# Second block of a two-block network: the context's first norm moved into the sums over V, and attention handled by head pairs

## The chip, the core and the metric

The kernel runs on one core of a Trainium2 chip, in one launch. The metric is the time of that launch on the device in microseconds, as the median of several runs; lower is better. TensorE (PE) multiplies matrices into PSUM, VectorE (DVE) and ScalarE (ACT) work element by element, GpSimd (POOL) issues the gathers and SyncE (SP) issues all other DMAs.

## The reference, cut to what matters

The network is one block (delta rule, dilated attention, and a feed-forward of 16384 experts) on 512 tokens of width 1024, followed by a second block of two layers, on the same tokens and on a context of 256 tokens. In float32 throughout. The change touches the hand-over between the blocks and the attention of the second one:

```python
# first block, its end: 128 chosen experts per token, kept as one dense sum over all experts
h = h + peer_ffn(rmsnorm(h, norm_ffn[layer]), ...)      # gelu(x U) * gates, then times V
# second block, layer i
h  = rms_norm(x,  norm_mix[i]) * (1.0 + sc1)  + sh1
hc = rms_norm(xc, norm_mix[i]) * (1.0 + sc1c) + sh1c    # xc: the context, 256 tokens
y, yc = token_mixers(h, hc, ...)
# token_mixers: gated linear attention (4 heads), and for each of 6 + 6 heads of width 64
s_loc = einsum(q, k of the window) * scale + bias       # neighbourhood (na) or sliding window (swa)
s_ctx = einsum(q, k of the context) * scale
p = softmax(concatenate([s_loc, s_ctx]))                # swa: with a sink
o = p_loc @ v of the window + p_ctx @ v of the context
```

## The kernel before, in words

Activations lie with features on the 128 partitions and tokens along the row. A projection is 8 chunks of 128 features times three matmuls (`mm3`, L204 to L206): operands are split into a high and a low part, and the three large products are summed in a PSUM bank `ac`. A weight tile of 512 KB is loaded (`wr`), its high part made on ACT (`wh`, L142) and its low part on DVE (`wl`, L199).

The stages around the change, in order: the sums over V (`peer_v`, 128 steps of 18 matmuls, with `sparse_v` on gathered rows beside them); a tail that turns the sums (`py`) round and adds them to `x`; then `ctx0`, the context's mixers in layer 0; `wo0c`, their output projection; `mix0`, the mixers of the 512 tokens; output projection and feed-forward; and `ctx1`, `mix1` and the rest for layer 1. In `ctx1` no attention output is needed.

In `block2`, `ctx0` begins with `s.norm`: for each of 8 chunks a scale on DVE (`nt`), a shift on ACT (`xh`) and the remainder on DVE (`xl`), on 256 columns. Its inputs, the context `cx`, its reciprocal norm `early_r` and the modulation `mod[0, 1]`, have been ready since the first block. `mixers` then runs generators side by side with `interleave`: each yields an estimate of TensorE's time and a gap before it is to go on, and the generator that is due next is asked next. A scheduler in the tile framework orders the instructions of each engine from that. The generators of `mixers` are one for the gated linear attention, three that take attention units from a queue, one for the projections (a next pair of heads waits until `aq.done` says that all but two pairs are through), and, in `ctx0`, `x_entry` (two norms of `x`, the first begins with the matmul at L267) and `mods`: 48 loads `mw` of 512 KB, each used by 8 matmuls of 32 weight columns (L1165).

One attention unit is one head and one block of 128 queries (`attn_unit`): scores (L1321 to L1325), `softmax` on DVE, ACT, DVE into `pr`, then `probs_times_v`: transposes (L236), a copy on ACT into `pt`, and one product per 128 keys (L410), 64 weight columns wide, into one half of the partitions of the bank `po`:

```python
        for j in range(nb):
            s.nc.tensor.matmul(po, vs[j], pt[:, j, :], start=j == 0, stop=j == nb - 1, skip_group_check=True)
```

A unit has nb = 2 blocks of keys in `ctx0`, 4 in neighbourhood attention, and 4 (first and last query block) or 5 in sliding-window attention. There are 24 units in `ctx0` and 48 each in `mix0` and `mix1`. After all mixers the outputs are split, and the output projection follows; TensorE's order takes its first products in between the last units.

Of the kernel before, what the change touches and what calls it, by code (L numbers as in the profile page):

```python
# [23 lines left out]
CTX = 256  # L24
# [18 lines left out]
def flat(t):  # L43
    return t.rearrange("p a b -> p (a b)")
# [61 lines left out]
class Net:  # L106
# [984 lines left out]
    def peer_v(s, p0, p1, x, Hd, Gd, S, sv, keep):  # L1091
# [38 lines left out]
        interleave([sv, reload(), dense()])  # L1130
# [57 lines left out]
    def gla(s, p, T, L, pair, s0, sout, y):  # L1188
# [9 lines left out]
        for d in range(2):  # L1198
# [113 lines left out]
    def attn_unit(s, p, q, loc, ctx, sink, vs, po, after=None):  # L1312


        mm = s.nc.tensor.matmul
        lw = loc[2] if loc else 0
        b0 = s.bank()
        cps = b0[:, lw:lw + CTX] if lw + CTX <= 512 else s.bank()[:, :CTX]
        segs = [(cps, s.zero[:, 0:1].to_broadcast([128, CTX]), lw)]
        if loc:  # L1320
            mm(b0[:, :lw], q, loc[0], start=True, stop=False)  # L1321
            mm(b0[:, :lw], q, loc[1], start=False, stop=True)
            segs.append((b0[:, :lw], loc[3](), 0))
        mm(cps, q, ctx[0], start=True, stop=False)
        mm(cps, q, ctx[1], start=False, stop=True)  # L1325
# [4 lines left out]
        if after:  # L1330
            after()
# [38 lines left out]
    def mixers(s, st, i, T, xp, xh, xl, y, is_ctx, lanes=()):  # L1370
# [9 lines left out]
        def units(kind, n, make):  # L1380

            box = {"left": n}

            def po():
                if "b" not in box:
                    box["b"] = s.pob()
                return box["b"]

            def after():
                box["left"] -= 1  # L1390
                if box["left"] == 0:
                    make["out"](box["b"])
            for g in make["units"](po, after):
                aq.put(g)
# [22 lines left out]
        def na_units(pair, ks, vw, qs, ck):  # L1417
            def mk(po, after):
                for n in range(nt):
                    nb = None  # L1420
                    if not is_ctx:
                        nb = {}
                    for h in range(2):
                        hh = slice(64 * h, 64 * h + 64)
                        cv = [KV["nv"][:, j, pair * 128 + 64 * h:pair * 128 + 64 * h + 64] for j in range(2)]
                        o = lambda n=n, hh=hh: po()[hh, n * 128:(n + 1) * 128]
                        q = qs[h][:, n * 128:(n + 1) * 128]
                        if is_ctx:
                            yield s.attn_unit(p, q, None, ks[h], None, cv, o, after)
                            continue  # L1430
                        w0 = (0, 64, 192, 256)[n]

                        def bias(n=n, h=h, nb=nb):
                            if "t" not in nb:
                                nb["t"] = s.t(p, "nbias", [128, 2, 256], 2)
                                nc.sync.dma_start(nb["t"], s.I["nabias"][i, n, :, 2 * pair:2 * pair + 2, :])
                            return nb["t"][:, h]
                        vs = [vw[:, n, j, hh] for j in range(2)] + cv
                        yield s.attn_unit(p, q, (ks[h][0][:, w0:w0 + 256], ks[h][1][:, w0:w0 + 256], 256, bias),
                                          ck[h], None, vs, o, after)  # L1440
            return mk

        def swa_units(pair, ks, vt, qs, ck):
            def mk(po, after):
                for n in range(nt):
                    for h in range(2):
                        head = 2 * pair + h
                        kv = head // 3
                        hh, vh = slice(64 * h, 64 * h + 64), slice(64 * kv, 64 * kv + 64)
                        cv = [KV["sv"][:, j, vh] for j in range(2)]  # L1450
                        q = qs[h][:, n * 128:(n + 1) * 128]
                        o = lambda n=n, hh=hh: po()[hh, n * 128:(n + 1) * 128]
                        sk = s.sink[:, head:head + 1]
                        if is_ctx:
                            yield s.attn_unit(p, q, None, ks[kv], sk, cv, o, after)
# [3 lines left out]
                        yield s.attn_unit(p, q, (ks[kv][0][:, lo * 128:hi * 128], ks[kv][1][:, lo * 128:hi * 128], w,  # L1459
                                                 lambda c0=c0, w=w: s.c2["swam"][:, c0:c0 + w]), ck[kv], sk,  # L1460
                                          [vt[:, j, vh] for j in range(lo, hi)] + cv, o, after)
# [4 lines left out]
        def proj_lane():  # L1466
            for kind, m in seq:
# [3 lines left out]
                if kind in ("nk", "sq") and y is not None:  # L1471
                    left = aq.put_pairs - 2
                    yield lambda left=left: aq.done >= left * 2 * nt
# [48 lines left out]
                elif kind == "nq":  # L1522
                    pair = m - 9
                    qs = s.q_parts(p, s.evac(p, ps, "ra", T, bufs=2, scale=0.125, grid=not is_ctx), T, "qp")
                    units(kind, 2 * nt, dict(units=na_units(pair, A["k"], A["v"], qs, A.get("ck")),
# [18 lines left out]
                elif kind == "sq":  # L1544
# [3 lines left out]
                    units(kind, 2 * nt, dict(units=swa_units(pair, A["sk"], A["sv"], qs, A.get("sck")),  # L1548
# [13 lines left out]
        interleave([gq.lane(), aq.lane(), aq.lane(), aq.lane(), *lanes, proj_lane()])  # L1562
# [133 lines left out]
    def block2(s, x):  # L1696
# [3 lines left out]
        with ExitStack() as st:  # L1700
# [11 lines left out]
            with ExitStack() as t:  # L1712
                s.mark("ctx0")
                xc, np_ = s.pool(t, "xc"), s.pool(t, "np")
# [3 lines left out]
                ch = s.norm(np_, xc, cx, mc[0][:, 8:16], CTX, mc[0][:, 0:8], s.early_r)  # L1718
                with ExitStack() as t2:
                    s.mixers(t2, 0, CTX, xc, *ch, cx, True, [s.x_entry(np_, x, gain, xp, mx[0], xs),  # L1720
# [7 lines left out]
                s.early_r = s.rstd(s.early, CTX)  # L1728
            for i in range(2):
# [194 lines left out]
def network(st, tc, I):  # L1924
# [5 lines left out]
    s.early = s.pool(st, "early")  # L1930
# [20 lines left out]
```

## Time and profile before

| | |
|---|---|
| median of 3 runs | 4083.6 us (4079.09 to 4084.34) |
| the profiled execution | 4080.38 us, its span 4078.6 us |
| TensorE busy | 3921.0 us, 96% of the span |
| VectorE busy | 2324.0 us, 57% |
| ScalarE busy | 1573.6 us, 39% |
| mean granted TensorE clock | 0.988 of full speed |

Busy is the time in which an engine had at least one instruction under way. Matmuls overlap, so the distance from one start to the next is what a matmul costs in a stream, not its own duration. A product of two float32 operands that were not split stands in the trace as two records (two passes). In the second block the stages lie at about 2228 to 2400 us (`ctx0`), 2400 to 2424 (`wo0c`), 2424 to 2713 (`mix0`), 3305 to 3385 (`ctx1`) and 3385 to 3656 (`mix1`).

### The profile page before, as it was taken

To read this page: it belongs to the slowest core of one execution; us is meant where nothing else is said; L and a number is where in the kernel's file an instruction comes from. 1 tells how busy PE (TensorE), PEld (TensorE's weight loads), DVE (VectorE), ACT (ScalarE), POOL (GpSimd) and SP (SyncE) were. 2 spreads that over 40 slices of the span, in tenths; PEclk is the share of its full clock that TensorE was granted. 3 is DMA by queue.
4 is the path that set the end of the run, shared out by engine and by line. 5 is a ranking of instruction groups with operands and counts; after the bars stand their busy time and mean duration, and the time that the engine had idled before them with its cause. 6 is when DMAs were issued, how large, how long until landed. Compare 5 with 4: busy or idle time off the path is not lost.

```text
span 4078.6 us, 57929 instructions
## 1 busy us (share of the span) xinstructions
PE 3921.0 (96%) x22491; PEld 3316.5 (81%) x22491; DVE 2324.0 (57%) x5133; ACT 1573.6 (39%) x2776; POOL 325.7 (8%) x287
## 2 busy tenths in 40 slices
PE   8999999999878999989998999999999999999998
PEld 5878988789877899766887778888888888887887
DVE  7526544569998776434556757663222266664334
ACT  5335454433223333323333645553121245553222
POOL 0000000004445310222000000000000000000000
PEclk9999999999998999999999999999999999999999
DMA  5342132338889876988764651121212141122332
GB/s 196 106 150 74 37 99 98 113 115 321 316 293 326 319 266 236 339 287 308 257 217 163 241 198 43 58 83 63 67 63 62 60 127 58 55 86 78 95 96 83
DMA packets 218594, 637.62 MB, mean 156 GB/s; under 512 B 25552, under 2 KB 65360, under 8 KB 214736
## 3 DMA queue, kind: packets, MB, share of 16 engines
q1 hardware_dynamic: 181456, 499.69, 36.3%
q0 software_dynamic: 36864, 134.23, 9.1%
q8 instruction: 177, 2.90, 0.3%
q14 instruction: 97, 0.79, 0.1%
HBM read 575.12 MB, written 58.72 MB: 155 GB/s over the span
## 4 chain that ended last, share of the span: by engine, by line
PE 54%; DMA 8%; DVE 6%; issue 1%; ACT 1%; POOL 0%; DVEq 0%; SPq 0%; ACTq 0%; POOLq 0%
PE ac L205 13%; PE ac L206 13%; PE ac L204 13%; DMA pa<-Hd 6%; PE po L410 3%; PE bk L995 2%; DVE wl L199 2%; PE bk L236 2%; PE bk L205 1%; PE bk L204 1%; PE bk L206 1%; DVE pl L145 1%; DMA wr<-V 1%; PE bk L1321 1%; PE bk L1165 1%
## 5 line engine op out<-in xcount | busy, mean ns | idle before, releaser
L204 PE MATMUL ac<-xh,wh 128*128 128x512 f32 (+2 forms) x3608 | 1301.6, 362 | 54.2 <-ACT h L136 41.2
L206 PE MATMUL ac<-xh,wl 128*128 128x512 f32 (+2 forms) x3608 | 1280.8, 356 | 14.1 <-DVE wl L199 13.8
L205 PE MATMUL ac<-xl,wh 128*128 128x512 f32 (+2 forms) x3608 | 1282.0, 356 | 1.0 <-DVE xl L148 0.7
L142 ACT ACTIVATE wh<-wr 128x1024 fp32r<-128x1024 f32 (+1 forms) x599 | 630.4, 1054 | 1618.9 <-PE ac L205 1173.4
L199 DVE TENSOR_TENSOR wl<-wr,wh 128x1024 fp32r<-128x1024 f32 (+1 forms) x599 | 726.9, 1214 | 557.4 <-ACT wh L142 529.8
L204 PEld LDWEIGHTS ac<-xh,wh 128*128 128x128 f32 x3608 | 683.8, 190 | 160.5 <-ACT h L136 51.7
L206 PEld LDWEIGHTS ac<-xh,wl 128*128 128x128 f32 x3608 | 683.8, 190 | 96.4 <-DVE wl L199 20.7
L205 PEld LDWEIGHTS ac<-xl,wh 128*128 128x128 f32 x3608 | 684.7, 190 | 79.8 <-issue 7.8
L145 DVE TENSOR_TENSOR pa<-pa,pg 128x384 f32<-128x384 f32 x128 | 66.1, 555 | 298.1 <-DMA pa<-Hd 292.0
L205 PE MATMUL bk<-wl,ph 128*128 128x512 f32 x512 | 201.2, 393 | 0.0
L204 PE MATMUL bk<-wh,ph 128*128 128x512 f32 x512 | 201.1, 393 | 0.0
L206 PE MATMUL bk<-wh,pl 128*128 128x512 f32 x512 | 200.6, 392 | 0.0
L205 PE MATMUL ac<-al,wh 128*128 128x512 f32 (+1 forms) x528 | 186.0, 352 | 0.0
L206 PE MATMUL ac<-ah,wl 128*128 128x512 f32 (+1 forms) x528 | 185.5, 351 | 0.0
L204 PE MATMUL ac<-ah,wh 128*128 128x512 f32 (+1 forms) x528 | 185.0, 350 | 0.0
L148 DVE SCALAR_TENSOR_TENSOR x<-ac,mod,x 128x512 f32<-128x512 f32 (+1 forms) x64 | 46.4, 726 | 186.1 <-PE ac L206 185.8
L993 DVE TENSOR_SCALAR ob<-iota,pi,pi 128x128 f32<-128x128 f32 x384 | 110.2, 350 | 72.7 <-PE bk L995 70.0
L915 POOL DMA_INDIRECT x<-Ur,rows x86 | 121.5, 1413 | 329.1 <-DVE sc L825 213.1
L145 DVE TENSOR_TENSOR nt<-ac,nt 128x512 f32<-128x512 f32 (+1 forms) x44 | 29.9, 680 | 160.2 <-PE ac L206 159.9
L142 ACT ACTIVATE ph<-pa 128x384 fp32r<-128x384 f32 x128 | 66.7, 523 | 138.8 <-DVE pa L145 61.9
L205 PE MATMUL ac<-wl,ph 128*128 128x512 f32 x256 | 101.9, 398 | 18.7 <-DVE wl L199 18.7
L915 POOL DMA_INDIRECT x<-V,rowsT x86 | 97.0, 1128 | 236.1 <-PE bk L956 212.4
(450 smaller groups left out, 5820.9 us busy)
## 6 DMA issues: line engine op xcount, KB each, us to landing
wr<-win SPq DMA_DIRECT2D x151, 512.0 KB, 3.5
wr<-U SPq DMA_DIRECT2D x128, 512.0 KB, 5.4
wr<-V SPq DMA_DIRECT2D x128, 512.0 KB, 5.8
mw<-wmod SPq DMA_DIRECT2D x96, 512.0 KB, 4.2
Hd<-h SPq DMA_DIRECT2D x64, 384.0 KB, 4.9
pa<-Hd SPq DMA_DIRECT2D x64, 384.0 KB, 5.9
Gd<-gs SPq DMA_DIRECT2D x24, 1024.0 KB, 7.5
pg<-Gd SPq DMA_DIRECT2D x21, 1152.0 KB, 7.2
```

Of the source, the lines that this page charges most:

```text
L142: s.nc.scalar.activation(out, in_, AF.Copy, **kw)
L145: s.nc.vector.tensor_tensor(out, a, b, op=op)
L148: s.nc.vector.scalar_tensor_tensor(out, a, sc, b, op0=op0, op1=op1)
L199: (eng or nc.vector).tensor_tensor(lo[:, :nk, :], raw[:, :nk, :], r32(hi[:, :nk, :]), op=ALU.subtract)
L204: mm(out, ah, bh, start=start, stop=False)
L205: mm(out, ah, bl, start=False, stop=False)
L206: mm(out, al, bh, start=False, stop=stop)
L236: s.nc.tensor.transpose(out, in_, s.ident)
L410: s.nc.tensor.matmul(po, vs[j], pt[:, j, :], start=j == 0, stop=j == nb - 1, skip_group_check=True)
L915: s.nc.gpsimd.indirect_dma_start(out=g, out_offset=None, in_=table, in_offset=bass.IndirectOffsetOnAxis(ap=idx, axis=0))
L993: nc.vector.tensor_scalar(a2, iota, iT[1][:, tok:tok + 1], iT[2][:, tok:tok + 1], op0=ALU.is_equal, op1=ALU.mult)
L995: nc.tensor.matmul(b[:, i * 128:(i + 1) * 128], a1[:, i], a2, start=True, stop=True)
```

## The change

Two edits. First, the context's norm is made by `norm_lane` as a third generator beside the sums over V, into a pool `xc` that is allocated at the right end of SBUF and freed after `wo0c`; `block2` only uses its result `s.ch`. Second, an attention unit now holds both heads of a pair for one query block: both heads' scores and softmaxes, then for two blocks of keys at a time four transposes into one bank, one copy, and four products, whose heads alternate. The heads' products write the lower and the upper 64 partitions of `po`. The bank is cleared first by a product with a zero weight (`make["some"]` is any tile of keys), and all products add. Two generators take units instead of three, `pr` has four buffers instead of three, `pt` holds two key blocks of both heads in three buffers, and `gqi` shares the buffer of `gla`.

```diff
@@ peer, peer_v
+            s.xc = s.ctx_stack.enter_context(s.tc.tile_pool(name="xc", bufs=1, side="right"))
             s.peer_v(v0, s.pool(st, "pv1"), x, Hd, Gd, S, sv, keep)
-        interleave([sv, reload(), dense()])
+        s.ch, mc = [], s.mod[0, 1]
+        interleave([sv, reload(), s.norm_lane(p1, s.xc, s.cx, mc[:, 8:16], CTX, mc[:, 0:8], s.early_r, s.ch), dense()])
@@ gla
-                qin = s.t(p, "gqi", [128, T], 1)
+                qin = s.t(p, "gla", [128, T], 1)
@@ attn_unit -> attn_pair
-        pr = s.t(p, "pr", [128, 640], 3)
-        s.softmax(pr, segs, sink)
-        yield (lw + CTX) * 2 * COL, 3.2
-        yield from s.probs_times_v(p, pr, vs, po())
+        for q, loc, ctx, sink, vs in heads:
...
+            pr = s.t(p, "pr", [128, 640], 4)
+            s.softmax(pr, segs, sink)
+            prs.append(pr)
+            yield (lw + CTX) * 2 * COL, 1.0
+        yield 0.0, 2.2
+        nb = len(heads[0][4])
+        out = po()
+        for j0 in range(0, nb, 2):
+            js = range(j0, min(nb, j0 + 2))
+            b = s.bank()
+            pt = s.t(p, "pt", [128, 4, 128], 3)
+            n = 2 * len(js)
+            for j in js:
+                for h in range(2):
+                    c = 2 * (j - j0) + h
+                    s.transpose(b[:, c * 128:(c + 1) * 128], prs[h][:, j * 128:(j + 1) * 128])
+            s.copy(flat(pt[:, :n, :]), b[:, :n * 128])
+            yield n * 0.11, 0.9
+            for j in js:
+                for h in range(2):
+                    mm(out[64 * h:64 * h + 64], heads[h][4][j], pt[:, 2 * (j - j0) + h, :], start=False,
+                       stop=j == nb - 1, skip_group_check=True)
+            yield n * 0.13, 0.0
+        after()
@@ mixers, units.po
                     box["b"] = s.pob()
+                    nc.tensor.matmul(box["b"][:, :T], s.zero.bitcast(F32R), make["some"], start=True, stop=False,
+                                     skip_group_check=True)
@@ mixers
-        interleave([gq.lane(), aq.lane(), aq.lane(), aq.lane(), *lanes, proj_lane()])
+        interleave([gq.lane(), aq.lane(), aq.lane(), *lanes, proj_lane()])
@@ block2
-                ch = s.norm(np_, xc, cx, mc[0][:, 8:16], CTX, mc[0][:, 0:8], s.early_r)
```

On TensorE, at the start of `ctx0`, the last turning of the sums (L236, `py`), the first matmul of `x_entry` (L267) and the first projections (`ac`) stood like this before:

```order
L236 MATMUL bk_18478<-ident,py_18407 128x128 x4
L267 MATMUL bk_18586<-na_18422,ones 128x512
L204 MATMUL ac_18617<-xh_18543,wh_14226 128x256
L205 MATMUL ac_18617<-xl_18544,wh_14226 128x256
L206 MATMUL ac_18617<-xh_18543,wl_14227 128x256
L204 MATMUL ac_18617<-xh_18543,wh_14226 128x256
L205 MATMUL ac_18617<-xl_18544,wh_14226 128x256
```

In the changed kernel both first projections, 48 matmuls, stand between the last L236 and L267, and this is the end of the second one:

```order
L206 MATMUL ac_18656<-xh_14258,wl_14236 128x256
L204 MATMUL ac_18656<-xh_14258,wh_14235 128x256
L205 MATMUL ac_18656<-xl_14259,wh_14235 128x256
L206 MATMUL ac_18656<-xh_14258,wl_14236 128x256
L267 MATMUL bk_18586<-na_18459,ones 128x512
L204 MATMUL ac_18698<-xh_14258,wh_18652 128x256
L205 MATMUL ac_18698<-xl_14259,wh_18652 128x256
```

So L267 moved behind two projections.

On TensorE, in the neighbourhood attention of `mix0`, the products with V (L410, out of `pt` and the values `nvw` and `knv`) of one head stood together:

```order
L236 MATMUL bk_23392<-ident,pr_23338 128x128 x4
L236 MATMUL bk_23401<-ident,pr_23355 128x128 x4
L1321 MATMUL bk_23411<-nkh_4251_23089,qp_4290_23296 128x256
L1322 MATMUL bk_23411<-nkl_4252_23090,qp_4290_23296 128x256
L1324 MATMUL bk_23411<-ckh_4247_23077,qp_4290_23296 128x256
L410 MATMUL po_23390<-pt_23391,nvw_23187 64x128 x2
L410 MATMUL po_23390<-pt_23391,knv_18524 64x128 x2
```

In the changed kernel the same place has both heads of a pair (`pr_22859`, `pr_22942`) by turns, and four products (L1353) of both heads in a row:

```order
L236 MATMUL bk_23034<-ident,pr_22859 128x128
L236 MATMUL bk_23034<-ident,pr_22942 128x128
L236 MATMUL bk_23034<-ident,pr_22859 128x128
L236 MATMUL bk_23034<-ident,pr_22942 128x128
L1353 MATMUL po_22777<-pt_22997,nvw_21861 64x128 x4
L236 MATMUL bk_23049<-ident,pr_22859 128x128
L236 MATMUL bk_23049<-ident,pr_22942 128x128
```

The transposes and the products alternate between the heads. The products with V form 106 separate runs in the whole second block, where they formed 121.

On TensorE, in the last part of neighbourhood attention in `mix0`, matmuls of the output projection (`ac_23576`, `ac_23604`) stood between the units before:

```order
L206 MATMUL ac_23576<-xh_23299,wl_23203 128x512
L410 MATMUL po_23390<-pt_23443,nvw_23187 64x128 x2
L410 MATMUL po_23390<-pt_23443,knv_18524 64x128 x2
L205 MATMUL ac_23604<-xl_23300,wh_23572 128x512
L206 MATMUL ac_23604<-xh_23299,wl_23573 128x512
L204 MATMUL ac_23604<-xh_23299,wh_23572 128x512
L205 MATMUL ac_23604<-xl_23300,wh_23572 128x512
L236 MATMUL bk_23468<-ident,pr_23416 128x128 x4
```

In the changed kernel most of those matmuls stand earlier, and the last eight query blocks of the pairs have next to none between them:

```order
L1353 MATMUL po_23123<-pt_23222,nvw_22539 64x128 x4
L236 MATMUL bk_23250<-ident,pr_23213 128x128
L236 MATMUL bk_23250<-ident,pr_23185 128x128
L1353 MATMUL po_23123<-pt_23229,nvw_22539 64x128 x4
L236 MATMUL bk_23250<-ident,pr_23213 128x128
L1353 MATMUL po_23123<-pt_23240,knv_18561 64x128 x4
L1327 MATMUL bk_23280<-nkh_4187_22894,qp_4209_23005 128x256
L1328 MATMUL bk_23280<-nkl_4188_22895,qp_4209_23005 128x256
L1330 MATMUL bk_23280<-ckh_4183_22882,qp_4209_23005 128x256
L1331 MATMUL bk_23280<-ckl_4184_22883,qp_4209_23005 128x256
```

So the projection's matmuls, which need no softmax, moved out of this stretch.

## Rows read from the trace of the kernel before

**Rows 1.** The page: busy time of TensorE, and the chain that ended last, by line.

```profile
PE 3921.0 (96%) x22491; PEld 3316.5 (81%) x22491; DVE 2324.0 (57%) x5133; ACT 1573.6 (39%) x2776; POOL 325.7 (8%) x287
...
PE ac L205 13%; PE ac L206 13%; PE ac L204 13%; DMA pa<-Hd 6%; PE po L410 3%; PE bk L995 2%; DVE wl L199 2%; PE bk L236 2%; PE bk L205 1%; PE bk L204 1%; PE bk L206 1%; DVE pl L145 1%; DMA wr<-V 1%; PE bk L1321 1%; PE bk L1165 1%
```

**Rows 2.** Windows, all instructions: stretch, its length, busy PE, PEld, DVE, ACT, POOL, clock, DMA.

```profile
1616.00:1640.00 24.00, 18.75 (x85) 11.79 (x82) 10.18 (x15) 7.12 (x9) 10.39 (x9) 1.00 1.00 361
...
2204.00:2228.00 24.00, 17.24 (x92) 14.69 (x91) 13.71 (x22) 6.18 (x11) 0.00 (x0) 0.91 0.16 49
2228.00:2240.00 12.00, 9.68 (x61) 7.39 (x63) 11.86 (x26) 8.01 (x18) 0.00 (x0) 0.90 0.59 201
...
2390.00:2400.00 10.00, 7.29 (x68) 5.02 (x67) 3.35 (x5) 3.26 (x5) 0.00 (x0) 0.88 0.85 280
...
2424.00:2713.00 289.00, 285.46 (x1794) 236.48 (x1792) 182.26 (x526) 156.18 (x315) 0.00 (x0) 1.00 0.19 60
3385.00:3656.00 271.00, 267.44 (x1707) 221.35 (x1705) 176.15 (x518) 149.60 (x305) 0.00 (x0) 0.99 0.18 56
```

**Rows 3.** Windows, tile `po` only: busy PE, PEld, ACT, then clock and DMA.

```profile
2227.00:2400.00 173.00, 15.22 (x96) 9.19 (x96) 2.29 (x6) 0.97 0.67 236
2424.00:2713.00 289.00, 54.18 (x408) 42.80 (x408) 3.59 (x6) 1.00 0.19 60
3385.00:3656.00 271.00, 54.58 (x408) 43.20 (x408) 3.59 (x6) 0.99 0.18 56
```

**Rows 4.** Timeline of TensorE: start, duration, instruction, records; units of 2, 5, 4 key blocks.

```profile
2377.86 0.65 PE L410 MATMUL po<-pt,knv 128*64 128x128 f32 x4
2378.44 0.44 PE L236 MATMUL bk<-ident,pr 128*128 128x128 f32 x2
...
2488.25 0.87 PE L410 MATMUL po<-pt,svt 128*64 128x128 f32 x6
...
2489.49 0.43 PE L1265 MATMUL bk<-gqi,kS 128*128 128x64 f32 x2
...
2633.96 1.09 PE L1271 MATMUL bk<-gat,gvt 128*64 128x128 f32 x16
2634.88 0.60 PE L410 MATMUL po<-pt,nvw 128*64 128x128 f32 x4
2635.32 0.60 PE L410 MATMUL po<-pt,knv 128*64 128x128 f32 x4
2635.85 0.38 PE L1321 MATMUL bk<-nkh,qp 128*128 128x256 f32 x1
```

**Rows 5.** Timeline of TensorE in `ctx0`: a run in which two heads' products met.

```profile
2296.84 0.66 PE L410 MATMUL po<-pt,ksv 128*64 128x128 f32 x8
2297.43 0.63 PE L1165 MATMUL bk<-mw,modl 128*32 128x256 f32 x6
```

**Rows 6.** Timeline of TensorE: start of `ctx0`, in brackets idle time before and releaser.

```profile
2227.50 2.05 PE L267 MATMUL bk<-na,ones 128*128 128x512 f32 x2 [6.76 <-DVE na L145]
...
2230.54 0.28 PE L204 MATMUL ac<-xh,wh 128*128 128x256 f32 x1
2230.66 0.28 PE L205 MATMUL ac<-xl,wh 128*128 128x256 f32 x1
...
2238.29 0.39 PE L204 MATMUL ac<-xh,wh 128*128 128x256 f32 x1 [1.02 <-ACT za L1478]
```

**Rows 7.** Windows 2227 to 2238, tile `nt` only: busy PE, PEld, DVE, ACT.

```profile
2227.00:2238.00 11.00, 0.00 (x0) 0.00 (x0) 6.66 (x16) 3.62 (x8) 0.84 0.59 202
```

**Rows 8.** Timeline: TensorE and SyncE at the end of `ctx0`.

```profile
2370.92 20.76 SPq L1162 DMA_DIRECT2D mw<-wmod  x12
...
2396.64 0.64 PE L1165 MATMUL bk<-mw,modl 128*32 128x256 f32 x8 [1.85 <-DMA mw<-wmod]
```

**Rows 9.** Timeline: one head's softmax, from its last scores (TensorE) to `pr` (VectorE).

```profile
2639.28 0.28 PE L1325 MATMUL bk<-ckl,qp 128*128 128x256 f32 x1
...
2642.02 0.49 DVE L396 TENSOR_SCALAR pr<-pr,sv 128x512 f32<-128x512 f32 x1
```

**Rows 10.** Windows 2595 to 2672 (12 heads' softmaxes), tile `pr` only: PE, PEld, DVE, ACT.

```profile
2595.00:2672.00 77.00, 6.08 (x44) 4.94 (x44) 16.35 (x36) 9.66 (x24) 1.00 0.21 62
```

More of the change, by code (lines that the diff above doesn't have):

```diff
@@ L1310, in k_parts, with attn_pair @@
         return out
-    def attn_unit(s, p, q, loc, ctx, sink, vs, po, after=None):
+    def attn_pair(s, p, heads, po, after):
         mm = s.nc.tensor.matmul
[L1316 to L1325, printed above, removed]
-        pr = s.t(p, "pr", [128, 640], 3)
-        s.softmax(pr, segs, sink)
-        yield (lw + CTX) * 2 * COL, 3.2
-        yield from s.probs_times_v(p, pr, vs, po())
-        if after:
-            after()
+        prs = []
+        for q, loc, ctx, sink, vs in heads:
+            lw = loc[2] if loc else 0
+            b0 = s.bank()
+            cps = b0[:, lw:lw + CTX] if lw + CTX <= 512 else s.bank()[:, :CTX]
+            segs = [(cps, s.zero[:, 0:1].to_broadcast([128, CTX]), lw)]
+            if loc:
+                mm(b0[:, :lw], q, loc[0], start=True, stop=False)
+                mm(b0[:, :lw], q, loc[1], start=False, stop=True)
+                segs.append((b0[:, :lw], loc[3](), 0))
+            mm(cps, q, ctx[0], start=True, stop=False)
+            mm(cps, q, ctx[1], start=False, stop=True)
+            pr = s.t(p, "pr", [128, 640], 4)
[22 more added lines that the diff above has]
+        after()
@@ L1419, in mk, with bias @@
                 for n in range(nt):
-                    nb = None
-                    if not is_ctx:
-                        nb = {}
+                    nb, w0 = {}, (0, 64, 192, 256)[n]
+                    def bias(h, n=n, nb=nb):
+                        if "t" not in nb:
+                            nb["t"] = s.t(p, "nbias", [128, 2, 256], 2)
+                            nc.sync.dma_start(nb["t"], s.I["nabias"][i, n, :, 2 * pair:2 * pair + 2, :])
+                        return nb["t"][:, h]
+                    heads = []
                     for h in range(2):
@@ L1425, in mk @@
                         cv = [KV["nv"][:, j, pair * 128 + 64 * h:pair * 128 + 64 * h + 64] for j in range(2)]
-                        o = lambda n=n, hh=hh: po()[hh, n * 128:(n + 1) * 128]
                         q = qs[h][:, n * 128:(n + 1) * 128]
                         if is_ctx:
-                            yield s.attn_unit(p, q, None, ks[h], None, cv, o, after)
+                            heads.append((q, None, ks[h], None, cv))
                             continue
[L1431 to L1440, printed above, removed]
+                        loc = (ks[h][0][:, w0:w0 + 256], ks[h][1][:, w0:w0 + 256], 256, lambda h=h, b=bias: b(h))
+                        heads.append((q, loc, ck[h], None, [vw[:, n, j, hh] for j in range(2)] + cv))
+                    yield s.attn_pair(p, heads, lambda n=n: po()[:, n * 128:(n + 1) * 128], after)
             return mk
@@ L1445, in mk @@
                 for n in range(nt):
+                    heads = []
                     for h in range(2):
@@ L1458, in mk @@
                         c0, w = (lo - n + 1) * 128, (hi - lo) * 128
-                        yield s.attn_unit(p, q, (ks[kv][0][:, lo * 128:hi * 128], ks[kv][1][:, lo * 128:hi * 128], w,
-                                                 lambda c0=c0, w=w: s.c2["swam"][:, c0:c0 + w]), ck[kv], sk,
-                                          [vt[:, j, vh] for j in range(lo, hi)] + cv, o, after)
+                        loc = (ks[kv][0][:, lo * 128:hi * 128], ks[kv][1][:, lo * 128:hi * 128], w,
+                               lambda c0=c0, w=w: s.c2["swam"][:, c0:c0 + w])
+                        heads.append((q, loc, ck[kv], sk, [vt[:, j, vh] for j in range(lo, hi)] + cv))
+                    yield s.attn_pair(p, heads, lambda n=n: po()[:, n * 128:(n + 1) * 128], after)
             return mk
@@ L1472, in proj_lane @@
                     left = aq.put_pairs - 2
-                    yield lambda left=left: aq.done >= left * 2 * nt
+                    yield lambda left=left: aq.done >= left * nt
                 ps = s.proj(s.w(), xh, xl, 8, T)
@@ L1524, in proj_lane @@
                     qs = s.q_parts(p, s.evac(p, ps, "ra", T, bufs=2, scale=0.125, grid=not is_ctx), T, "qp")
-                    units(kind, 2 * nt, dict(units=na_units(pair, A["k"], A["v"], qs, A.get("ck")),
+                    units(kind, nt, dict(units=na_units(pair, A["k"], A["v"], qs, A.get("ck")), some=A["k"][0][0],
                                              out=(out_plain if is_ctx else out_grid)(2 + pair)))
@@ L1547, in proj_lane @@
                     qs = s.q_parts(p, src, T, "qp")
-                    units(kind, 2 * nt, dict(units=swa_units(pair, A["sk"], A["sv"], qs, A.get("sck")),
+                    units(kind, nt, dict(units=swa_units(pair, A["sk"], A["sv"], qs, A.get("sck")), some=A["sk"][0][0],
                                              out=out_plain(5 + pair)))
@@ L1728, in block2 @@
                 s.early_r = s.rstd(s.early, CTX)
+            s.ctx_stack.close()
             for i in range(2):
```

11 lines of the change are left out of this document (5 added, 6 removed).

## The prediction

> **What bounds the kernel now.** I read the page's busy times first, then its chain, then the second block stage by stage, then single rows. TensorE is busy 96% of the span, and the chain that ended last names its matmuls above all; the products with V (`po`, L410) have 3% of the span in it by themselves [rows 1]. The windows say the same of the stages that change: in `mix0` it works 285.46 of 289 us, in `mix1` 267.44 of 271, while VectorE works 182 and 176, ScalarE 156 and 150 [rows 2]. So in the mixers a matmul that goes away is time that goes away, as long as VectorE and ScalarE still deliver `pr` and `pt` in time. Three places are not of this kind: the hand-over at 2204 to 2240, where TensorE idles [rows 2]; the end of `ctx0`, where it waits for a load of `mw` [rows 8]; and the start of the sums over V, where the DMA engines are busy all the time and TensorE works 18.75 of 24 us [rows 2].
>
> **Products with V.** I cost them by the distance from a unit's first product to the next other matmul [rows 4]. A unit of two key blocks takes 2378.44 - 2377.86 = 0.58 us, of five 2489.49 - 2488.25 = 1.24, of four 2635.85 - 2634.88 = 0.97. The 24 units of `ctx0` have two; of 96 units in the mixes 48 are neighbourhood attention (four), 24 are the edge blocks of the sliding window (four), and 24 its middle blocks (five). That is 24 x 0.58 + 72 x 0.97 + 24 x 1.24 = 113.5 us. The rows of tile `po` check it: 15.22 + 54.18 + 54.58 = 124 us busy [rows 3], more, since each run's last matmul ends later than the next one starts.
>
> What two heads by turns cost, two rows show. In `ctx0` two units happened to meet, and four products on both halves of the bank took 2297.43 - 2296.84 = 0.59 us [rows 5]: as much as two on one half. And L1271 alternates heads already: eight products of the same shape took 2634.88 - 2633.96 = 0.92 us, where two units of L410 with four each take 1.94 [rows 4]. So products on the two halves run side by side. After the change there are 108 full groups of four products (12 in `ctx0`, 48 in each mix) and 12 groups of two (the fifth key block). At 0.59 the first make 63.7 us. A group of two, one on each half, lies between nothing and 0.58 (two on one half); nearest are the rows of four, of which it is half, and with a fixed part I take 0.40: 4.8 us. After: 68.5, saved 45.0 us (6.8 in `ctx0`, 19.1 in each mix). Were each group of four as dear as four on one half, 0.97, it would save nothing worth the name; were they 0.46 each, as in L1271, 59 us.
>
> The Trainium skill ("TensorE: Matmul & The Clock Gate", Part 2) says that a weight load is pulled ahead of running matmuls where the row groups don't conflict or where it goes to the background buffer; both heads here use all 128 rows, so read strictly the first condition fails, and the pairs would bring nothing by it. The rows on L1271 and the chance meeting speak against that reading; the skill's "TensorEngine Tiling (Array Packing)", Key Properties, has tiles of 64 columns run independently, with which they agree.
>
> **The clearing product.** 18 of them: 6 of 256 columns, 12 of 512. A matmul of 256 columns takes 2230.66 - 2230.54 = 0.12 us in a stream [rows 6]; 512 columns twice that. 6 x 0.12 + 12 x 0.24 = 3.6 us (0.7 in `ctx0`, 1.4 in each mix). Net: `ctx0` -6.1, each mix -17.7 us.
>
> **The norm, where it was.** After the last turning of `py`, TensorE waits 6.76 us for `na` before L267. The first two projections come only then, and last from 2228.56 to 2238.29, some 10 us [rows 6], since VectorE first makes `nt` and `xl`, one after the other; the granted clock is 0.90 there, where `mix0` has 1.00 [rows 2]. Their 48 matmuls are 48 x 0.12 = 5.8 us of work. In the changed order they stand before L267, with `xh` and `xl` made long before, so they fit into the idle 6.76 us. That takes away the 10 us. Against it: VectorE now makes two `wl` between the additions of `na`, about 1.2 us each, by which L267 comes later. At the later end the same operands of `x` are awaited by nobody in `ctx0`. So -10 + 2.4 = about -7; at most -9, and -4 if the next weights are late.
>
> **The norm, where it goes.** 16 operations of VectorE (6.66 us) and 8 of ScalarE (3.62 us) [rows 7] run among the first steps of the sums over V. There the loads bind (DMA at 1.00), VectorE works 10.18 and ScalarE 7.12 of 24 us [rows 2]; there is room. But a weight's split that waits behind them holds its buffer longer, and so the next load. Below nothing is excluded, above it is the 6.66 + 3.62 us in full, less what TensorE idles: 0 to 9. I take +1, since both engines idle more than half of that stretch.
>
> **The end of `ctx0`.** The last twelve `mw` are issued over 20.76 us, 1.73 us each, and at the end TensorE waits 1.85 us for one [rows 8]; DMA is at 0.85 in the last 10 us [rows 2]. The changed order leaves 17 to 18 of these loads for the last stretch, as attention there is through sooner. A faster TensorE waits for them, and they give back part of the 6.1 + 7 us that `ctx0` won: between 0 (the queue also starts earlier) and 10; I take +5. Behind a late `mw` stands only the modulation, and `wo0c` after it.
>
> **The ends of neighbourhood attention in the mixes.** A head's softmax takes 2642.51 - 2639.28 = 3.2 us from its last scores to `pr` [rows 9]. For 12 heads VectorE spends 16.35 us on `pr` and ScalarE 9.66 [rows 10]: 1.36 and 0.80 us a head. In the old order the output projection's matmuls stand between the last units and fill TensorE; in the new one the last eight query blocks have next to none. There one block of two heads costs VectorE 2 x 1.36 = 2.7 us, more with the small operations on one column, and TensorE some 3.0 us (before about 3.8). So it is close, and every first block in that stretch waits for a whole softmax chain, 3.2 us. Least: 1 us; most: 8 blocks with 0.9 us each, two chains of 3.2: 14. I take +6.5 in each mix, two chains.
>
> **The sum.** -6.1 - 7 + 5 + 1 + 2 x (-17.7 + 6.5) = -29.5 us. Against the profiled execution (4080.38 us, its span 4078.6) this is 4051. That execution lies 3.2 us below the median of the runs shown, 4083.6; I keep 4051, as the runs lie closer to it at the fast end.
>
> **The rivals.**
>
> *The halves do not run side by side.* Then groups of four cost 0.97, and the products make 108 x 0.97 + 12 x 0.58 = 111.7 us instead of 113.5. With the clearing, the norm, 3 us at the end of `ctx0`, the sums over V and the ends of the mixes this gives -1.8 + 3.6 - 7 + 3 + 1 + 2 x 6.5 = +12: 4092, and 4081 with 1 us at each end. Against it speak both rows of products by turns [rows 4, 5]. Chance 0.04. (It is what the Trainium skill's rule on row groups, cited above, would come to here.)
>
> *Softmax becomes the bound: slower.* Both heads of a block go in step, and only two lanes are left, so a chain of two softmaxes, transposes and a copy is in flight at most twice. If TensorE waits for `pr` or `pt` in all of attention and not only in the last blocks, each of the 60 pair blocks (24 in a mix, 12 in `ctx0`) pays; from 29.5 / 60 = 0.49 us per block, beyond what I count already, the change turns slower. At 1 us it is 4051 + 60 = 4111. For it: the chain of 3.2 us against 3.0 us of work. Against it: projections, linear attention and `mw` stand between in most of the stretch, and VectorE is at 63% [rows 2]. Chance 0.06.
>
> *`ctx0` is bound by its loads.* What it wins is given back, all 13 us, by waits for `mw`; the mixes remain: 4080.4 + 1 - 22.4 = 4059. Chance 0.2.
>
> *The ends of the mixes cost nothing.* The lane of the linear attention fills them; 4051 - 11 = 4040. Chance 0.17.
>
> *The sums over V are held up* by the full 9 us: 4059. Chance 0.08.
>
> **How the numbers follow.** The forecast (each term near its value) has 0.45. Faster by over 0.2% (8 us, about what a measurement of this kernel can tell from no change) is all but the first two rivals and a tail of the load-bound case joined with dear ends: 0.86. Same: 0.08, slower: 0.06. The range goes from 4033, the ends at 1 us and products half way to 0.46 (-11 and -7), to 4073, loads and ends at the upper bounds: -6.1 - 4 + 10 + 3 + 2 x (-17.7 + 7) = -18.5, and some way to the first rival.
>
> **What the profile would show.** Right: products of `po` in runs of eight records with 0.59 us to the next matmul, and `po` busy near 33 us in each mix instead of 54; the first projection before L267 and the idle time before L267 down to about 2 us or less; waits for `mw` at the end of `ctx0`; waits of transposes for `pr` and of products for `pt` only in the last third of each mix; the stretch of the sums over V as long as before. Wrong: groups of four at 0.9 us, waits for `pr` or `pt` summed over a mix above 15 us, or first steps of the sums over V later than before by more than a few us.

## The result, and the profile after

The changed kernel takes 4057.1 us (median of 4 runs, 4053.6 to 4062.9), the kernel before 4082.9 beside it; the ratio is 0.994, with a 95% interval of 0.9922 to 0.9957. A second series gave 4054.9 against 4083.4, ratio 0.9933 (0.9917 to 0.9949). The forecast was 4051 in a range of 4033 to 4073. The profiled execution is the slowest of its four, 4062.9 us with a span of 4061.1.

The page of the changed kernel, busy times and chain, as in [rows 1]:

```profile
PE 3887.4 (96%) x22509; PEld 3274.3 (81%) x22509; DVE 2327.0 (57%) x5133; ACT 1569.4 (39%) x2752; POOL 329.9 (8%) x287
...
PE ac L205 11%; PE ac L206 11%; PE ac L204 11%; DMA pa<-Hd 3%; PE bk L236 2%; PE po L1353 2%; DVE wl L199 1%; PE bk L1168 1%; PE bk L204 1%; PE bk L205 1%; PE bk L206 1%; PE bk L1268 0%; DVE pr L386 0%; DVE pl L145 0%; PE bk L1327 0%
```

TensorE is 34 us less busy, but the span is only 17.5 us shorter than that of [rows 1]'s profile: part of what was saved came back as waiting, some of it in the sums over V, which took 14.5 us longer in this profile. The starts of marking instructions in the traces say where. The table is worked out from them, in us. "V": from the first matmul of the sums to the first turning of `py`. "Hand-over": from the last turning until L267 and the first 48 projection matmuls are over. "Rest of ctx0": from there to the L267 that ends `wo0c`. "mix0": to its last product with V. "ffn0": from the first L286 behind that product to the L267 behind ffn0. "ctx1, mix1": from there to the last product with V.

| profile of | V | hand-over | rest of ctx0 | mix0 | ffn0 | ctx1, mix1 |
|---|---|---|---|---|---|---|
| before | 600.6 | 17.8 | 184.4 | 288.0 | 555.2 | 351.1 |
| before, once more | 606.1 | 17.8 | 181.7 | 288.0 | 555.1 | 350.9 |
| after | 615.1 | 10.0 | 176.1 | 283.0 | 548.5 | 346.3 |
| after, once more | 602.8 | 9.9 | 172.5 | 283.3 | 556.0 | 346.2 |
| norm's edit alone | 616.3 | 9.9 | 179.5 | 288.0 | 555.1 | 351.1 |
| pairs alone | 610.6 | 17.8 | 176.5 | 283.2 | 556.0 | 345.2 |
| no wait for `pr` | 604.9 | 10.0 | 175.7 | 267.7 | 555.1 | 330.1 |
| queries later | 604.1 | 9.9 | 171.5 | 268.2 | 555.2 | 330.4 |

The columns V and ffn0 differ between two profiles of one kernel as much as between kernels. The rest of `ctx0` repeats to 4 us, the other columns to 0.3 us.

The timeline of TensorE in the changed kernel, a group of four products and what follows it, to be read against [rows 4, 5]:

```profile
2300.23 0.66 PE L1353 MATMUL po<-pt,ksv 128*64 128x128 f32 x8
2300.82 0.39 PE L206 MATMUL ac<-xh,wl 128*128 128x256 f32 x1
```

The group costs 2300.82 - 2300.23 = 0.59 us, as forecast; over all 74 groups of the changed kernel that stand alone the median is 0.59 too. The windows of tile `po` alone answer to [rows 3] (busy PE, PEld, ACT, then clock and DMA):

```profile
2227.00:2400.00 173.00, 9.45 (x102) 6.16 (x102) 2.26 (x6) 0.95 0.69 243
2419.00:2704.00 285.00, 36.92 (x414) 23.58 (x414) 3.58 (x6) 0.98 0.20 63
3386.00:3636.00 250.00, 37.59 (x414) 24.20 (x414) 3.57 (x6) 0.97 0.18 55
```

Busy with `po` falls by 5.8, 17.3 and 17.0 us, the six clearing products of each stage included, which are 2.5 us of the busy time after in each mix.

At the hand-over (timeline of TensorE, in brackets the idle time before and its releaser; compare [rows 6]):

```profile
2229.41 3.66 PE L236 MATMUL bk<-ident,py 128*128 128x128 f32 x32
2232.83 0.36 PE L204 MATMUL ac<-xh,wh 128*128 128x256 f32 x1
...
2238.45 0.28 PE L206 MATMUL ac<-xh,wl 128*128 128x256 f32 x1
2241.72 2.05 PE L267 MATMUL bk<-na,ones 128*128 128x512 f32 x2 [2.99 <-DVE na L145]
```

The 48 matmuls run without a stop right behind the turnings, 2232.83 to 2238.45, and 2.99 us of the old 6.76 us of idle time are left.

The waits of TensorE in `mix0` by releaser: us in total, times, longest. Before:

```profile
PE bk L236 <- DVE pr L396: 2.7, 4, 1.8
PE po L410 <- ACT pt L142: 0.4, 1, 0.4
PE bk L236 <- DVE sv L390: 0.2, 1, 0.2
```

After:

```profile
PE bk L236 <- DVE pr L396: 7.1, 5, 2.3
PE bk L204 <- ACT wh L142: 1.6, 1, 1.6
PE po L1353 <- ACT pt L142: 1.0, 3, 0.4
PE bk L1327 <- DVE sv L386: 0.8, 1, 0.8
```

The wait for the softmax has more than doubled (that for `wh` lies behind the last product with V). What it draws after it is in the windows of 5 us at the end of `mix0` of the changed kernel (busy PE, PEld, DVE, ACT, POOL, granted clock, DMA):

```profile
2655.00:2660.00 5.00, 2.16 (x10) 1.23 (x8) 4.87 (x23) 2.29 (x6) 0.00 (x0) 1.00 0.10 19
2660.00:2665.00 5.00, 4.59 (x27) 3.49 (x29) 2.37 (x8) 2.71 (x7) 0.00 (x0) 0.66 0.28 88
2675.00:2680.00 5.00, 3.55 (x34) 2.59 (x30) 3.57 (x19) 1.95 (x6) 0.00 (x0) 1.00 0.01 3
2680.00:2685.00 5.00, 4.53 (x28) 3.90 (x29) 2.70 (x10) 3.09 (x7) 0.00 (x0) 0.66 0.33 105
2695.00:2700.00 5.00, 2.63 (x32) 2.02 (x29) 2.38 (x9) 1.77 (x5) 0.00 (x0) 1.00 0.02 3
2700.00:2705.00 5.00, 2.95 (x24) 2.10 (x22) 2.03 (x4) 3.81 (x7) 0.00 (x0) 0.65 0.00 0
2705.00:2710.00 5.00, 5.00 (x24) 4.41 (x23) 3.90 (x7) 2.99 (x5) 0.00 (x0) 0.67 0.45 157
```

Three times TensorE is busy for 2 to 3.6 of 5 us, and each time the 5 us behind it run at a mean granted clock of 0.65 or 0.66, that is two thirds of them at 1.2 GHz instead of 2.4. Before, all of `mix0` had 1.00 [rows 2]. The third slow stretch lies behind the mix, in the output projection, where it goes on at 0.67, for this is the last product with V of `mix0`:

```profile
2701.28 0.95 PE L1353 MATMUL po<-pt,knv 128*64 128x128 f32 x8
```

### The profile page after: what moved, and what is told of

The parts are those of the page before. It is cut to its first block, busy times and chain, and to the rows that moved or that the text cites. A ratio compares the mean times of both kernels' runs of the same rounds, so it can differ in the third digit from the quotient of the medians.

```text
span 4061.1 us, 57874 instructions
## 1 busy us (share of the span) xinstructions
PE 3887.4 (96%) x22509; PEld 3274.3 (81%) x22509; DVE 2327.0 (57%) x5133; ACT 1569.4 (39%) x2752; POOL 329.9 (8%) x287
## 4 chain that ended last, share of the span: by engine, by line
PE 42%; DVE 4%; DMA 3%; ACT 1%; issue 1%; DVEq 0%; ACTq 0%
PE ac L205 11%; PE ac L206 11%; PE ac L204 11%; DMA pa<-Hd 3%; PE bk L236 2%; PE po L1353 2%; DVE wl L199 1%; PE bk L1168 1%; PE bk L204 1%; PE bk L205 1%; PE bk L206 1%; PE bk L1268 0%; DVE pr L386 0%; DVE pl L145 0%; PE bk L1327 0%
```

## The experiments

**Twice the same kernels.** The changed kernel and the kernel before, as they are.

> The changed kernel once more, for a second profile of it. In its first profile the sums over V took 615 us from their first product to the first turning of py (before: 601), and ffn0 ran 584 to 585 matmuls in 100 us (before: 578). Theory 1: both vary from one execution to the next, the change has no part in them; then here the sums over V take anything from 600 to 615 us, and ffn0 may run 578 again. Rival: both belong to the change; then again 612 to 618 us and 584 to 585 matmuls. Time 4057, as measured.

> The kernel before once more, for a second profile of it. Theory 1 (chance): the sums over V may take anything from 600 to 615 us, ffn0 may run 584 matmuls in 100 us. Rival (belongs to the change): 598 to 603 us and 578 matmuls, as in the first profile. Time 4083.

Measured: 4054.9 us (ratio 0.9933) and 4081.6 (one run). The sums over V took 602.8 us in the second profile of the changed kernel and 606.1 in that of the kernel before. One window of ffn0 in the first and in the second profile of the changed kernel:

```profile
3040.00:3140.00 100.00, 100.00 (x585) 87.95 (x584) 29.51 (x38) 17.22 (x22) 0.00 (x0) 1.00 0.21 64
```

```profile
3040.00:3140.00 100.00, 100.00 (x578) 88.02 (x577) 28.88 (x36) 16.39 (x21) 0.00 (x0) 1.00 0.20 64
```

So both vary from one execution of the same kernel to the next. That the change has no part in how often is not shown: the shorter ffn0 stands in three of ten profiles with the pairs and in none of four without. Over all profiles the sums over V took 606.6 us on average in ten executions with the norm in them (602.4 to 616.3) and 605.9 in four without (600.6 to 610.6): the norm's new place costs less than can be told here.

**One edit at a time.** `norm_only` is the kernel before with the lines on `s.xc`, `norm_lane` and `s.ch`; `pairs_only` is the changed kernel with them taken back:

```diff
-        interleave([sv, reload(), s.norm_lane(p1, s.xc, s.cx, mc[:, 8:16], CTX, mc[:, 0:8], s.early_r, s.ch), dense()])
+        interleave([sv, reload(), dense()])
...
+                ch = s.norm(np_, xc, cx, mc[0][:, 8:16], CTX, mc[0][:, 0:8], s.early_r)
```

> The kernel before with the norm's edit alone; attention head by head as before. Theory 1: the norm gives the 7.8 us by which the first two projections and the norm of x are over sooner after py, and nothing else of it matters: 4083 - 8 = 4075, the sums over V as long as in other profiles of the kernel before. Rival: the norm costs 14 us in the sums over V, by its operations or its pool, and gives 6.7 us in ffn0 by the moved pool: 4083 - 7.8 + 14.6 - 6.7 = 4083.

> The changed kernel with the norm back at the start of ctx0; attention by pairs. Theory 1: ctx0 gives 5.7 us by its products and some 2.6 by shorter waits, each mix 3.6: 4083 - 15.5 = 4067. Rival: the pairs bring all that the changed kernel brings, and the norm nothing: 4057. In both, each mix is 285 to 287 us long instead of 289, with TensorE waiting for pr in its last third.

Measured: 4070.3 us, ratio 0.9966 (0.9955 to 0.9978), and 4069.9, ratio 0.9959 (0.9945 to 0.9973). The two gains, 13.1 and 13.5 us, add up to 26.6, about what both edits bring together, so they do not get in each other's way. The norm alone is 5 us faster than its expectation. By the table it gives 7.9 us at the hand-over and, against the mean of the two profiles of before, 3.5 in the rest of `ctx0`, where two profiles of one kernel lie 2.7 and 3.6 us apart. The pairs give 6.5 us in `ctx0`, 4.8 in `mix0` and 5.8 in the last column; a mix is shorter than the 285 to 287 us expected. They give some of it back in the output projections, 1.3 us each (37.2 us between the last product and the L286 before ffn, 35.9 before).

**What the ends of the mixes cost.** In neighbourhood attention of both mixes the transposes read the identity:

```diff
-                    s.transpose(b[:, c * 128:(c + 1) * 128], prs[h][:, j * 128:(j + 1) * 128])
+                    s.transpose(b[:, c * 128:(c + 1) * 128], (s.ident if nb == 4 and heads[0][1] and heads[0][3] is None else prs[h][:, j * 128:(j + 1) * 128])[:, :128])
```

> The changed kernel, where the transposes of the neighbourhood attention of both mixes read the identity matrix instead of pr; the softmaxes are still made, but nobody there waits for them, and the output is not the reference's. Theory: at the ends of the mixes TensorE loses some 8 us by waiting for pr and some 5 us by the granted clock that falls behind the waits, in each mix; both go: 4056 - 2 x 13 = 4030, mix0 271 us instead of 283, granted clock 1.00 throughout. Rival: the ends of the mixes are bound by something else (the copies to pt, the products themselves, the clock in any case); then at most 2 x 3 us go: 4050 or more.

Measured: 4025.9 us, ratio 0.9861 (0.9847 to 0.9876). `mix0` took 267.7 us and the last column 330.1, which puts the price of the ends at 15.5 and 16.1 us. It is the price against a kernel without the dependence, not against the same order without its waits: from the first block of neighbourhood attention on, some 300 of the 1800 matmuls of `mix0` stand elsewhere on TensorE. Without the ends the pairs save 288.0 - 267.7 = 20.3 us in `mix0`.

**Useless work in the waits.** In the last 8 blocks of each mix:

```diff
+        if fill:
+            d = s.bank()
+            for _ in range(fill):
+                mm(d[:, :256], s.zero.bitcast(F32R), heads[0][1][0], start=True, stop=True)
         yield 0.0, 2.2
```

> The changed kernel with 12 matmuls of 256 columns and no use (zero weight, into a spare bank) between the scores and the transposes of each of the last 8 blocks of neighbourhood attention in both mixes: 8 x 12 x 0.12 = 11.5 us of work a mix that fills the waits for pr. Theory: of the 15 to 19 us that the ends of a mix cost, some 8 are waits and 5 to 8 are the granted clock that falls to half after them; with the filling the clock stays at 1.00, so that a mix gets 11.5 us of work more, loses 7 us of waits and 5 or more of slow clock, and is as long as before the filling or shorter: 4050 to 4058. Rival: the clock has no part in it, only the waits: 283 + 11.5 - 7 = 287 for mix0, 4063 to 4067 in all, or the clock falls to 0.66 in 5 us stretches all the same.

Measured: 4050.4 us, ratio 0.9934 (0.9918 to 0.995). `mix0` took 281.8 us and the last column 344.4, 1.2 to 1.9 us less than without the filling, with 11.5 us of work more in each mix. The same 5 us stretches:

```profile
2655.00:2660.00 5.00, 5.00 (x44) 4.96 (x43) 4.57 (x23) 3.04 (x8) 0.00 (x0) 1.00 0.42 120
2660.00:2665.00 5.00, 4.97 (x51) 3.63 (x49) 2.82 (x11) 2.98 (x6) 0.00 (x0) 1.00 0.11 40
2675.00:2680.00 5.00, 5.00 (x45) 5.00 (x44) 4.54 (x20) 2.86 (x8) 0.00 (x0) 1.00 0.38 105
2680.00:2685.00 5.00, 4.97 (x50) 3.63 (x49) 2.81 (x12) 2.98 (x6) 0.00 (x0) 1.00 0.00 0
```

The clock is at 1.00 throughout `mix0`. TensorE was idle for 10.6 us of `mix0` in the changed kernel (272.44 us busy of 283.0) and for 3.8 here (278.04 of 281.8), so the filling took the place of about 7 us of waits, yet 11.5 us of it cost less than nothing: the clock had its part. As a whole the kernel is not told from the changed one by this measurement.

**Work with a use in the waits.** One number, which lets a next pair's queries be projected later:

```diff
-                    left = aq.put_pairs - 2
+                    left = aq.put_pairs - 1
```

> The changed kernel, in which the projection of a next pair's queries waits until all but one pair are through, instead of all but two. By that, projections stand between the last pairs' blocks. Theory: what is missing at the ends of the mixes is work without softmax between the blocks; with it the waits for pr fall from 8 to 3 us and the clock holds: each mix 6 to 10 us shorter, 4056 - 16 = 4040. Rival: the later projection is itself waited for, by its rotation, its split and the scores behind it, and gives back what it fills: 4052 to 4062.

Measured: 4026.9 us, ratio 0.9865 (0.9847 to 0.9884). The waits of TensorE in `mix0`:

```profile
PE bk L204 <- ACT wh L142: 1.6, 1, 1.6
PE bk L236 <- DVE pr L396: 0.7, 2, 0.4
PE po L1353 <- ACT pt L142: 0.6, 2, 0.4
PE bk L1367 <- DVE sv L395: 0.4, 1, 0.4
```

`mix0` falls to 268.2 us and the last column to 330.4, half a microsecond from the kernel whose transposes do not wait for `pr`, and the clock of `mix0` is 1.00 again:

```profile
2409.00:2677.00 268.00, 265.76 (x1801) 215.02 (x1799) 182.58 (x530) 155.51 (x310) 0.00 (x0) 1.00 0.20 66
```

All that the ends cost is won back, and the gain of 28 us was even more than expected. Three further kernels mark its limits. The same edit in the kernel before (`before_late_q`), the same in the two mixes only (`- (2 if is_ctx else 1)`), and one step more (`left = aq.put_pairs`):

> The kernel before with the edit of late_q alone (a next pair's queries wait until all but one pair are through). Theory: late_q won its 29 us by filling waits that only the pairs brought; the kernel before waits for pr and pt for no more than 3 us in a mix and keeps its clock, so here the edit gives at most 4 us a mix: 4078 to 4084. Rival: the later projection is good by itself (it spreads the work of VectorE and ScalarE); then 4055 to 4065 here too.

> late_q in the two mixes only; ctx0 as in the changed kernel. Theory: all of late_q's gain lies in the mixes, since ctx0 has the loads of mw to stand between and its end is bound by them: 4025 to 4031 as late_q, ctx0 within 2 us of the changed kernel's. Rival: part of it came from ctx0 (its order changes too): 4032 or more.

> late_q by one step more: a next pair's queries wait until all pairs before are through. Theory: work is spread best where one pair's blocks are still there to stand between; one step more leaves the scores of each pair behind a projection that begins only when the pair before is through, so that the end of each pair has nothing beside it but the projection itself and waits for pr come back, some 2 us at each of the 5 changes of pairs in a mix: late_q's 4027 + 2 x 4 = 4035 or more, more than 4 us of waits for pr and pt in mix0. Rival: the later the better; 4015 to 4024.

Measured: 4075.3 us, ratio 0.9987 (0.9975 to 0.9999); 4029.5, ratio 0.9871 (0.9855 to 0.9886); 4052.4, ratio 0.9922 (0.9908 to 0.9935). The first is a little below its expectation (4078 to 4084) and far from the rival's. In the kernel before the edit takes 1.5 us off `mix0` and 2.4 off the last column; so most of what it gains above is the filling of waits that the pairs brought. Its gain lies in the mixes. And one step more goes too far, by 25 us: `mix0` takes 280.3 us and the last column 340.7, though not for the reason expected. Its waits for `pr` stay small, and projections wait instead for ScalarE:

```profile
2546.14 0.80 PE L204 MATMUL ac<-xh,wh 128*128 128x512 f32 x1 [2.71 <-ACT nvT L142]
2546.73 0.63 PE L205 MATMUL ac<-xl,wh 128*128 128x512 f32 x1
```

That wait and one of 1.7 us are 4.4 of the 12 us that `mix0` lost against `late_q`. The granted clock fell here too, twice:

```profile
2545.00:2550.00 5.00, 3.87 (x17) 3.67 (x18) 3.61 (x9) 2.80 (x5) 0.00 (x0) 0.66 0.32 105
2670.00:2675.00 5.00, 4.75 (x21) 4.08 (x22) 4.80 (x15) 4.57 (x10) 0.00 (x0) 0.71 0.54 203
2675.00:2680.00 5.00, 5.00 (x24) 4.05 (x24) 5.00 (x17) 1.40 (x4) 0.00 (x0) 0.95 0.64 200
```

That is (0.34 + 0.29 + 0.05) x 5 = 3.4 us of work not done. The rest, some 4 us, stays open.

**The order of the products, and the clearing.** First head by head within a group of four, then without the clearing product:

```diff
-            for j in js:
-                for h in range(2):
+            for h in range(2):
+                for j in js:
```

> The changed kernel with the four products of a group in another order: two of one head, then two of the other. Theory of the prediction (heads by turns run side by side): here only the middle two are neighbours on different halves, a group takes some 0.78 us instead of 0.59: 108 x 0.19 = 20 us on TensorE, less what the waits at the ends of the mixes swallow: 4056 + 14 = 4070. Rival: being next to each other is enough, the turns are not needed, as in the chance meeting of two units before the change, which stood in this order; then 0.59 us and 4056.

Measured: 4060.7 us, ratio 0.9949 (0.9935 to 0.9963), within what runs of the changed kernel scatter (4050.7 to 4067.5). A group head by head:

```profile
2302.74 0.66 PE L1353 MATMUL po<-pt,ksv 128*64 128x128 f32 x8
2303.34 0.39 PE L1330 MATMUL bk<-nkh,qp 128*128 128x256 f32 x1
```

It takes 0.60 us. The rival was right: to stand next to each other is enough. That the order on TensorE did change, the starts of the records show: they come in pairs in both kernels, the two of a pair 6 to 8 ns apart by turns and some 13 ns head by head.

```diff
-                    nc.tensor.matmul(box["b"][:, :T], s.zero.bitcast(F32R), make["some"], start=True, stop=False,
-                                     skip_group_check=True)
...
-                    mm(out[64 * h:64 * h + 64], heads[h][4][j], pt[:, 2 * (j - j0) + h, :], start=False,
+                    mm(out[64 * h:64 * h + 64], heads[h][4][j], pt[:, 2 * (j - j0) + h, :], start=j == 0,
```

> The changed kernel without the clearing product: each head's first product starts the sum in its half of the bank, as before the change. Theory: the 18 products of 0.12 to 0.43 us on TensorE cost 5 us in all, and what stands in the last part of the mixes is hidden by waits: 4056 - 3 = 4053. Rival: they cost nothing (a wait takes their place): 4056; or the clearing is what lets both halves run side by side, and without it a group of four takes 0.97 us instead of 0.59: 4056 + 20 = 4076 or more.

Measured: 4052.8 us, ratio 0.9934 (0.9917 to 0.995); `mix0` took 282.1 us and the last column 343.9, 1.2 and 2.3 us less than in the changed kernel's second profile. The clearing costs some 3.5 us in the two mixes, about as expected. It is a price and no version of the program: in places another query block's products stand between the first and the second group of a block, and their start flag falls into the same bank; the sums are no longer the reference's. The Trainium skill ("PSUM — Partial Sum Buffer", "PSUM: the matmul accumulator") says that of two open sums in the same bank and the same partitions not both may begin with the flag; this run agrees.

## Why the prediction came out right, and where it did not

The time and the sign were right; two of the terms were off by more than 5 us each, and in opposite directions. That the sum came within some 6 us is in part luck. By edits the forecast was 6 us for the norm and 28.5 for the pairs, less 5 us that both were to give back at the end of `ctx0`; alone they brought 13.1 and 13.5.

- **Products with V: right in mechanism and price.** 0.59 us a group. The groups of two, taken at 0.40, have 0.37 where they stand alone; the clearing products, taken at 3.6 us, have 5.2 to the next starts. `po` was to be busy for near 33 us in each mix and is for 36.9 and 37.6, the clearing included. The saving forecast for a mix was 19.1 us less 1.4 for the clearing, 17.7; `mix0` without waits is 20.3 us shorter. In `ctx0` 6.1 were forecast, and the pairs alone took 6.5 off it. What does not hold is a word: that the heads must come by turns. The records of the chance meeting of [rows 5] start in pairs 12 to 13 ns apart, as those of `by_head`. Of the two pages of the Trainium skill cited there, the runs agree with "TensorEngine Tiling (Array Packing)", Key Properties, by which different tiles work in parallel: both heads use all 128 rows, and still four products took 0.59 us.
- **The norm, where it was: right.** Forecast -7, measured -7.9. It removed 3.8 us of the idle time before L267 (2.99 are left, where about 2 or less were forecast) and the slow stretch behind it, and L267 does come later, 8.9 us after the start of the last turning instead of 7.0.
- **The norm, where it goes: not contradicted.** Forecast +1 within 0 to 9; the means of the profiles differ by 0.7 us, but single profiles scatter by some 5 us about them. That speaks against the upper bound and cannot tell the term from nothing.
- **The end of `ctx0`: wrong.** Forecast +5; the rest of `ctx0` is 8.8 us shorter on the mean of two profiles each, at least what the products save. TensorE waited for `mw` for 4.2 us in the first profile of either kernel and for 2.8 (before) and 3.8 us (after) in the second. Before, first profile:

```profile
PE bk L1165 <- DMA mw<-wmod: 4.2, 3, 1.8
PE ac L206 <- DVE wl L199: 1.6, 2, 1.0
PE bk L1324 <- DVE qp L145: 1.2, 3, 0.5
PE ac L204 <- DVE cx L148: 0.4, 1, 0.4
```

  After, first profile:

```profile
PE bk L1168 <- DMA mw<-wmod: 4.2, 4, 2.5
PE bk L267 <- DVE na L145: 3.0, 1, 3.0
PE ac L206 <- DVE wl L199: 0.2, 1, 0.2
```

  The loads kept up: the term's lower bound, 0, was the value to take. Besides, the waits for `wl`, `qp` and `cx` of VectorE fell from 3.2 to 0.2 us (0.9 in the second profile), for which the prediction had no term; with the 5.8 us less of `po` that makes up the 8.8.
- **The ends of the mixes: the step that failed.** Forecast +6.5 for each, with 14 as the upper bound; measured 15.5 and 16.1. The waits were of the size that the upper bound allows: in `mix0` those for `pr`, `pt` and `sv` above come to 7.1 + 1.0 + 0.8 = 8.9 us, those of `late_q` to 1.7; all idle time of TensorE in `mix0` is 10.6 us (272.44 busy of 283.0), and 3.0 in `no_wait` (264.72 of 267.7). What the term lacked is the clock: the two slow stretches within `mix0`, 5 us at 0.66 each, are (0.34 + 0.34) x 5 = 3.4 us of work not done. 7.6 + 3.4 = 11 us are so accounted for; some 4 us have no row. The third slow stretch costs as much again, (0.35 + 0.33) x 5 = 3.4 us, in the output projection, which is 1.3 us longer in all. So a mix gained 3.6 us (with its output projection) where 11.2 were forecast. Which part of the edit makes the waits, the two generators in place of three, the two heads in step or the projections that moved ahead, was not separated; `late_q` shows that work between the blocks removes them.

So the sum holds because 15 us that the two mixes did not give met 8.5 us that `ctx0` with the hand-over gave beyond the forecast. By stages the gain is 7.9 + 8.8 + 3.6 + 3.6 = 23.9 us; the medians differ by 25.8 and 28.5, and what is between lies within the scatter of V and ffn0. Of the rivals none came true, though the scatter of V does not let the last one be measured: softmax became the bound only in the last third of each mix, as the forecast had it, and not in all of attention.

## What to carry to other kernels

Count the work without a dependence that stands between dependent steps before you make TensorE's part of these steps cheaper: here products cheaper by 20 us a mix brought less than 4 us until one number moved the projections into the gaps, and the same number is worth little in the kernel before. Short waits are dearer than their own length where the granted clock falls behind them; read the clock in windows of a few us, not as a mean over the stage (0.98 here). And products of two heads that write different halves of the partitions need only be neighbours here: four took 0.59 us by turns and 0.60 head by head, as long as two on one half.

## What the runs showed of the hardware that was not expected

- **The same stream at two speeds.** ffn0 took 548.4 or 548.5 us in three of the fourteen profiles (the changed kernel once, `fill`, `late_q_mix`) and 555.0 to 556.0 in the others, at a granted clock of 1.00 in both. The changed kernel took both, 548.5 us in one profile and 556.0 in the other. The difference lies in the matmuls of 256 columns, which mostly follow each other at 113 ns in the one case and at 118 in the other; those of 512 keep their mean of 229. What sets it is open. A difference of 7 us between two single executions of this kernel therefore proves nothing.
- **The clock falls after waits that are each short.** No wait for `pr` was longer than 2.3 us, and still the granted clock fell three times in 45 us. The Trainium skill ("TensorE: Matmul & The Clock Gate", "HAM oscillation — how this bites in real kernels") describes such a fall after each wait for a load in a loop, with waits of some 3 to 5 us; these rows show it after shorter waits, for a softmax in the place of a load.
- **Products on two halves start in pairs.** In the 74 groups that stand alone in the changed kernel the eight records start two at a time, 6 to 8 ns apart, and from pair to pair it is mostly 160 ns and then 109. In the kernel before, on one half, each record of such a run starts alone, mostly 160 ns and then 109 behind the one before. Which record belongs to which head the trace does not say.
